# Encoder layer on one core: where a conditioning store is queued, the order of four prologue instructions, and the buffers of four rows at the end of the joint gate stage

## The chip, the core and the metric

The kernel runs on one NeuronCore of a Trainium2 chip. The core has TensorE (PE, matmuls; its weight loads are listed as PEld), VectorE (DVE), ScalarE (ACT), GpSimd (POOL) and SyncE (SP). SP issues most loads on a hardware queue (q1), POOL issues stores and some loads on a software queue (q0), ACT a few stores (q10). Three queues, sixteen DMA engines below them.

The metric is the device time of one execution in microseconds. A profiled execution adds a trace; its span is the time from its first to its last instruction.

## What is computed

One layer, width 1024, 1024 positions, everything float32 in and out:

```
mod = silu(c) @ w_ada + b_ada               # 6 columns of 1024: sh1 sc1 gt1 sh2 sc2 gt2
h   = rmsnorm(x, norm1_g) * (1 + sc1) + sh1
z   = h @ w_in                              # u v q k va gate_a gate_b
a   = gmlp(u, v) @ w_a;  b = window_attention(q, k, va) @ w_b
merged = sigmoid(gate_a) * a + sigmoid(gate_b) * b
x   = x + gt1 * (merged @ w_o)
h2  = rmsnorm(x, norm2_g) * (1 + sc2) + sh2
x   = x + gt2 * ((silu(h2 @ w_gate) * (h2 @ w_up)) @ w_out)
```

## The kernel before

**Numbers as pairs.** A float32 matrix product is made from pairs: a tile is cast to a rounded high part, and the low part is what the rounding left (`split`, `unit`). A product of two pairs is three matmuls: high by high, high by low, low by high. So each 128x1024 weight tile costs one cast on ACT (`wh<-raw`) and one subtraction on DVE (`wl<-raw,wh`) or POOL before PE can use it. The raw tile, the high part and the low part each have three buffers (tags `raw`, `wh`, `wl` of `wpool`).

**Who sets the order.** A planner turns the text into one instruction list for each engine. It lets an instruction run ahead of earlier text when its inputs and its buffer are there, unless the text pins it. `load` (line 137) issues a transfer from SP and pins it in SP's order. `store` (line 140) issues one from POOL and does not pin it; several loads go through `store` as well. Where `in_order[0]` is true, every DVE, ACT, POOL and PE instruction made through the wrappers stays in the order of the text. A tile that asks for a buffer of a tag waits until few enough earlier tiles of that tag are still in use.

**Prologue (lines 737 to 780, pinned).** The half of x that is worked on first comes in as eight 128x640 pieces (`xt`, `mid<-in_xT_dram`). ACT squares them, DVE sums the squares into `ss`, PE sums over partitions, ACT takes the square root (`root`, tile name `ms`), DVE takes its reciprocal (`rcol`), PE spreads it over partitions, and two ACT copies bring it to SBUF (`rb`, tile name `ss`). Meanwhile `silu_c` (the SiLU of c, repeated on all partitions) is there, and `ada_dot` (one 128x1024 DVE instruction) multiplies a 128x1024 row block of `w_ada` by it and sums: one column of `mod`. The blocks come in pairs of 1 MB (`ada_pair`), the scale's (SC1) in the first half and the shift's (SH1) in the second. `ada_end` is a one-column instruction that adds the bias.

**Projection loop (lines 795 to 854, pinned).** For each of eight k: scale `xt[k]` by the column of `mod` and by `rb` (DVE, 128x640), cast to a high part with the shift added (ACT), take the low part (DVE, `h<-mid,mod,h`), then the q and k/v matmuls of that k. Between them DVE makes the two dots of the next k, and in some steps the low part of a weight tile.

**Attention of the first half (lines 1052 to 1085).** Eight steps s, not pinned as a whole. In step 5 the text has the store of `silu_c` to `silu_d` in DRAM (512 KB, tile name `silu_d<-silu_c`), which the last stage of the kernel reads again.

**Joint gate stage (lines 1239 to 1327).** For each row block d = 2 to 7 the two sigmoid gates are computed with seven block products (`gate_step`, 12 matmuls each; after some of them `gate_evict` reads the sums) and `gating` writes two 128x512 results to DRAM, `md[0][d]` and `md[1][d]`. The two weight tiles of a d come in with `gate_load(d)` one d earlier and use two of the three `raw` buffers. During the stage `ada_half` streams further `w_ada` rows through the two buffers of the tag `hs`.

In its last row block, d = 7, the rows `md[0][0]` to `md[0][7]` are brought back as pairs for the output projection: `m_load` starts a load into an `hs` buffer through `store`, `m_split` casts and subtracts. Rows 0 and 1 are loaded first; each split of a row k in 0 to 3 starts the load of row k + 2; rows 6 and 7 need no load, since `gating` leaves them in SBUF. The splits of 0 to 3, 6 and the gating are pinned; those of 4, 5 and 7 are not. The first weight tile of the projection, `w_o[0]`, is asked for inside d = 7, and `w_o[1]` and on in the projection loop (lines 1345 on), where PE needs the rows 0 to 7 in order.

Of the kernel before, what the change touches and what calls it, by code (L numbers as in the profile page):

```python
# [8 lines left out]
F32 = mybir.dt.float32  # L9
# [7 lines left out]
P = 128  # L17
# [21 lines left out]
def kernel(  # L39
# [99 lines left out]
    def store(dst, src):  # L139
        nc.gpsimd.dma_start(dst, src)  # L140
# [66 lines left out]
    def ada_dot(r, col):  # L207
        V.scalar_tensor_tensor(
            out=r, in0=r, scalar=1.0, in1=silu_c, op0=ALU.mult, op1=ALU.mult,
            accum_out=acc_mod[:, col : col + 1],  # L210
        )

    def ada_end(col, gain=None):
        o = mod[:, col : col + 1]
        if gain is None:
            V.tensor_scalar(o, acc_mod[:, col : col + 1], bada[:, col : col + 1],
                            0.5 if GT1 <= col < SH2 else 1.0, op0=ALU.add, op1=ALU.mult)
        else:
            V.scalar_tensor_tensor(
                out=o, in0=acc_mod[:, col : col + 1], scalar=badap[:, col : col + 1],  # L220
                in1=gain, op0=ALU.add, op1=ALU.mult,
            )
# [509 lines left out]
    def half(hf):  # L732
# [4 lines left out]
        if hf == 0:  # L737
            in_order[0] = True
            xt = [midt(F32, 1) for _ in range(3)]
            xt = [xt[k // 3][:, 0, k % 3 * 640 : (k % 3 + 1) * 640] for k in range(KT)]  # L740
            hl4 = midt(F32R, 16)
            base_bias = bias_base()
            build_bias(*base_bias, range(7))
            A.activation(sm(QPK, "es"), ones[:, :QPK], AF.Silu)
            crow = load_cond()
            for k in range(KT):
                load(xt[k], xT[k * P : (k + 1) * P, :640])
            r = ada_pair(0)
            wq0, wk0 = raw_unit(w_q[0]), raw_unit(w_kv[0])
            cond = silu_rows(crow)  # L750
            ss = ss_tile()
            sqs = [midt(F32, 1)[:, 0, :] for _ in range(3)]
            for k in range(KT):
                sq = sqs[k // 3][:, k % 3 * 640 : (k % 3 + 1) * 640]
                A.activation(sq, xt[k], AF.Square)
                if k:
                    V.tensor_tensor(ss, prev if k == 1 else ss, sq, op=ALU.add)
                prev = sq
                if k == 1:
                    silu_cond(cond)  # L760
                    V.tensor_scalar(badap, bada, 1.0, None, op0=ALU.add)
                    build_bias(*base_bias, range(7, NH))
            total = at_bank()
            for i in range(NT + 1):
                T.matmul(total[:, i : i + 1], ss[:, i * P : (i + 1) * P], ones[:, 0:1], start=True,
                         stop=True)
            root = sm(5, "ms")
            A.activation(root, total[:, : NT + 1], AF.Sqrt, scale=1.0 / D, bias=epsc)
            ada_dot(r[:, 0, :], SC1)
            ada_end(SC1, g1c[:, 0:1])  # L770
            ada_dot(r[:, 1, :], SH1)
            V.reciprocal(rcol[0], root)
            wq = unit(None, V, wq0)
            wk = [wpool.tile([P, UNIT], F32R, tag=x, name=nm(x)) for x in ("wh", "wl")]
            A.copy(wk[0], wk0)
            r = ada_pair(1)
            ada_dot(r[:, 0, :], SC1 + 1)
            rb = ss_tile()
            A.copy(rb[:, :HALF], spread(rcol[0], NT))
            A.copy(rb[:, HALF:], spread(rcol[0][:, NT : NT + 1], 1))  # L780
            hH = [hid(), hid()]
            hL = [hid(), hid()]
        else:
            hH, hL = h_next
# [10 lines left out]
        for k in range(KT):  # L795
            if hf == 0:
                x = xt[k]
                h4 = hl4[:, k, :]
                sh = mod[:, SH1 + k : SH1 + k + 1]
                if 0 < k < KT - 1:  # L800
                    r = ada_pair(k + 1)
                V.scalar_tensor_tensor(out=x, in0=x, scalar=mod[:, SC1 + k : SC1 + k + 1], in1=rb,
                                       op0=ALU.mult, op1=ALU.mult)
                ada_end(SH1 + k)
                A.activation(hH[k // 4][:, k % 4, :], x[:, :HALF], AF.Identity, bias=sh)
                if k == 0:
                    V.tensor_tensor(wk[1], wk0, wk[0].bitcast(F32), op=ALU.subtract)
                A.activation(h4, x[:, HALF:], AF.Identity, bias=sh)
                A.activation(x[:, HALF:], x[:, HALF:], AF.Identity, bias=sh)
                G.tensor_tensor(hl4[:, KT + k, :], x[:, HALF:], h4.bitcast(F32), op=ALU.subtract)  # L810
                if 0 < k < KT - 1:
                    ada_dot(r[:, 0, :], SC1 + k + 1)
                V.scalar_tensor_tensor(out=hL[k // 4][:, k % 4, :], in0=x[:, :HALF], scalar=sh,
                                       in1=hH[k // 4][:, k % 4, :].bitcast(F32),
                                       op0=ALU.add, op1=ALU.subtract)
                if k < KT - 1:
                    ada_end(SC1 + k + 1, g1c[:, k + 1 : k + 2])
                    ada_dot(r[:, 1, :], SH1 + k + 1)
                store(x0d[k], x[:, :HALF])
                if k == 7:  # L820
                    for i in range(2):
                        x_square(i)
            else:
                if k == 0:
                    wq, wk = early.pop(0), early.pop(0)
            if k == 4:
                wk = unit(None, V, wk_raw)
            if k % 2 == 1 and k < KT - 1:
                wq_next = unit(w_q[(k + 1) // 2], V)
            if k == 3:  # L830
                wk_raw = raw_unit(w_kv[1])
            sts = [(hH[k // 4][:, k % 4, t * P : (t + 1) * P], hL[k // 4][:, k % 4, t * P : (t + 1) * P])
                   for t in range(NT)]
            ksts = sts + [(hl4[:, k, :], hl4[:, KT + k, :])] if hf == 0 else sts[1:]
            oq, ok = (k % 2) * 512, (k % 4) * 256
            q_parts = [(qps[t], sts[t], wq, oq, 512, True, True) for t in range(NT)]
            k_parts = [(kps[t], ksts[t], wk, ok, 256, hf == 1 or t == 4, hf == 1 or t % 2 or t == 4)
                   for t in range(nkv)]

            for group in ((q_parts, k_parts) if k == 4 else (q_parts + k_parts,)):  # L840
                for e in range(2):
                    for ps, st, w, o, n, first, last in group:
                        if e == 0:
                            T.matmul(ps, st[0], w[0][:, o : o + n], start=k == 0 and first, stop=False)
                            T.matmul(ps, st[0], w[1][:, o : o + n], start=False, stop=False)
                        else:
                            T.matmul(ps, st[1], w[0][:, o : o + n], start=False,
                                     stop=bool(k == KT - 1 and last))
            if hf == 1 and k in (2, 3):
                ada_half_load(("hs", "xs")[k % 2])  # L850
            elif hf == 1 and k > 3:
                ada_half(("hs", "xs")[k % 2] if k < 6 else None)
            if k % 2 == 1 and k < KT - 1:
                wq = wq_next
# [197 lines left out]
        for s in range(nw):  # L1052
# [8 lines left out]
            if hf == 0 and s == 7:  # L1061
                x_rstd()
            if hf == 0 and s == 5:
                store(silu_d, silu_c)
            normalise(sc[0], sc[2], den)
            if s == 0:
                end_unit()
# [172 lines left out]
    for d in range(2, KT):  # L1240
# [41 lines left out]
        if d > 2:  # L1282
            if last:
                m0.extend(m_tiles(midt))
                for k in range(2):
                    m_load(m0, 0, k)
                m_src[6] = tmp()
                gating(d - 1, None, m_src[6])
            else:
                gating(d - 1)  # L1290
# [5 lines left out]
        if not last:  # L1296
            gate_prep_a(d + 1)
        else:
            wo_next = unit(w_o[0], V)
            for k in (0, 1):  # L1300
                m_split(m0, k)
                m_load(m0, 0, k + 2)
        gate_step(d, 4)
        gate_evict(d, 4)
        if not last:
            gate_sums(d + 1)
            low_b, low_s = gate_prep_b(d + 1)
        else:
            m_split(m0, 6)
            for k in (2, 3):  # L1310
                m_split(m0, k)
                m_load(m0, 0, k + 2)
            m_src[7] = tmp()
            gating(d, 0, m_src[7])
        gate_step(d, 5)
# [666 lines left out]
```

## Time and profile before

| | |
|---|---|
| time, median of 3 runs | 1249.4 us (1247.3 to 1250.37) |
| the profiled execution | 1249.81 us |
| its span | 1248.0 us |
| granted TensorE clock | 1.000 |
| PE busy | 1219.6 us, 98% of the span |
| DVE busy | 915.1 us, 73% |
| ACT busy | 577.8 us, 46% |
| POOL busy | 184.0 us, 15% |
| DMA, mean over the span | 189 GB/s |

A row of the timeline is: start in us, duration in us, engine, line, operation, output and inputs by tile name, how many instructions are merged into the row, and in brackets the idle time before it and what ended that. Nearly all compute rows carry line 76, the wrapper that makes them, so they are told apart by tile names. A row of the waits is: who waited for whom, us in total, how many times, the longest. A row of the windows is: the stretch, its length, busy us (and instructions) of PE, PEld, DVE, ACT and POOL, the granted clock, the busy share of the DMA engines and the GB/s they moved.

### The profile page before, as it was taken

The numbers are of one execution on the slowest core, as the hardware profiler recorded it, in microseconds if no ns is written. First come the engines' busy times: TensorE is split into PE (matmuls) and PEld (weight loads), VectorE is DVE, ScalarE is ACT, GpSimd is POOL, SyncE is SP. The second block draws the span as 40 slices with busy tenths as digits, with TensorE's granted clock in tenths as the row PEclk, the third lists the DMA queues.
The fourth block names the chain that finished last, engine by engine and source line by source line (L and its number), as shares of the span: only waits on it lengthen the run. The fifth ranks groups of instructions, "written<-read, shape, count | busy, mean of one in ns | idle before, by whom it ended". The sixth has DMA issues, their size and how long they took to land.

```text
span 1248.0 us, 15657 instructions
## 1 busy us (share of the span) xinstructions
PE 1219.6 (98%) x5634; PEld 1008.8 (81%) x5634; DVE 915.1 (73%) x1548; ACT 577.8 (46%) x938; POOL 184.0 (15%) x234
## 2 busy tenths in 40 slices
PE   5999999999999999999999999999999999999998
PEld 3888888888887887788888887888888887888887
DVE  8997884487897798877797766765766666665746
ACT  5477864267876323434554333333333334433342
POOL 1223330023342010332100000010000000010001
PEclk9999999999999999999999999999999999999999
DMA  9721258431157466777503445455554459896642
GB/s 359 276 102 60 77 184 297 144 100 51 60 162 241 162 203 236 243 281 257 215 34 117 170 152 186 155 199 193 183 213 170 169 189 377 320 354 227 198 155 102
DMA packets 77664, 236.29 MB, mean 189 GB/s; under 512 B 9361, under 2 KB 9361, under 8 KB 71570
## 3 DMA queue, kind: packets, MB, share of 16 engines
q1 hardware_dynamic: 55298, 142.48, 32.9%
q0 software_dynamic: 18832, 86.52, 19.6%
q10 hardware_dynamic: 3456, 6.29, 1.3%
q8 instruction: 44, 0.72, 0.2%
q14 instruction: 34, 0.28, 0.1%
HBM read 177.58 MB, written 57.67 MB: 189 GB/s over the span
## 4 chain that ended last, share of the span: by engine, by line
PE 63%; DVE 12%; issue 11%; DMA 9%; ACT 3%; POOL 1%; SPq 0%; ACTq 0%; POOLq 0%; DVEq 0%
PE at L76 32%; PE mm L76 31%; DVE mid L76 3%; DVE wl L76 3%; ACT wh L76 2%; DMA wS<-wo 2%; DMA raw<-in_w_out_dram 1%; DMA raw<-in_w_ga_dram 1%; DMA wo<-in_w_out_dram 1%; DVE hs L76 1%; DMA mid<-in_w_ada_dram 1%; DVE t L76 1%; DVE ws L76 1%; DVE raw L76 1%; DVE xs L76 1%
## 5 line engine op out<-in xcount | busy, mean ns | idle before, releaser
L76 ACT CAST wh<-raw 128x1024 fp32r<-128x1024 f32 x155 | 162.4, 1051 | 146.5 <-PE mm L76 45.6
L76 DVE TENSOR_TENSOR wl<-raw,wh 128x1024 fp32r<-128x1024 f32 x141 | 171.9, 1221 | 71.1 <-ACT wh L76 68.4
L76 PE MATMUL mm<-mid,wh 128*128 128x512 f32 x696 | 215.7, 390 | 1.8 <-ACT mid L76 1.0
L76 PEld LDWEIGHTS mm<-mid,wh 128*128 128x128 f32 x696 | 130.3, 188 | 31.2 <-ACT mid L76 1.9
L76 PE MATMUL at<-j,wh 128*128 128x512 f32 x464 | 143.0, 389 | 0.0
L76 PE MATMUL mm<-mid,wl 128*128 128x512 f32 x348 | 135.4, 390 | 0.6 <-POOL wl L76 0.6
L76 PE MATMUL mm<-wh,h 128*128 128x512 f32 x384 | 128.8, 397 | 2.8 <-ACT h L76 2.7
L76 PEld LDWEIGHTS at<-j,wh 128*128 128x128 f32 x464 | 86.9, 188 | 18.5 <-ACT wh L76 0.4
L76 DVE TENSOR_TENSOR wl<-ws,wh 128x1024 fp32r<-128x1024 f32 (+1 forms) x55 | 62.0, 1127 | 43.9 <-ACT wh L76 43.9
L76 PE MATMUL at<-j,wl 128*128 128x512 f32 x232 | 90.4, 389 | 0.5 <-DVE wl L76 0.5
L76 PE MATMUL mm<-j,wh 128*128 128x512 f32 x288 | 89.0, 390 | 0.6 <-ACT wh L76 0.6
L76 PE MATMUL at<-h,wh 128*128 128x512 f32 x288 | 89.0, 390 | 0.0
L76 PEld LDWEIGHTS mm<-wh,h 128*128 128x128 f32 x384 | 71.2, 188 | 17.8 <-ACT h L76 4.1
L76 PE MATMUL mm<-h,wh 128*128 128x512 f32 x272 | 84.5, 392 | 0.0
L76 ACT CAST wh<-ws 128x1024 fp32r<-128x1024 f32 (+1 forms) x55 | 53.6, 974 | 59.3 <-DVE ws L76 43.5
L76 PEld LDWEIGHTS mm<-mid,wl 128*128 128x128 f32 x348 | 65.3, 188 | 14.4 <-POOL wl L76 1.0
L76 PE MATMUL mm<-wl,h 128*128 128x512 f32 x192 | 75.0, 391 | 0.0
L76 PEld LDWEIGHTS mm<-j,wh 128*128 128x128 f32 x288 | 53.8, 188 | 12.0 <-ACT wh L76 1.0
L76 PEld LDWEIGHTS at<-h,wh 128*128 128x128 f32 x288 | 53.8, 188 | 11.3 <-DVE mid L76 0.3
L76 PEld LDWEIGHTS mm<-h,wh 128*128 128x128 f32 x272 | 50.6, 188 | 10.3
L76 ACT ACTIVATE xs<-xs 128x512 f32<-128x512 f32 x21 | 13.3, 633 | 98.0 <-DVE xs L76 98.0
L76 DVE TENSOR_TENSOR ol<-raw,oh 128x1024 fp32r<-128x1024 f32 x30 | 36.5, 1223 | 27.8 <-ACT oh L76 27.3
(284 smaller groups left out, 2576.5 us busy)
## 6 DMA issues: line engine op xcount, KB each, us to landing
raw<-in_w_gate_dram SPq DMA_DIRECT2D x28, 512.0 KB, 5.1
tA<-hid POOLq DMA_DIRECT2D x11, 1024.0 KB, 4.9
tB<-hid POOLq DMA_DIRECT2D x11, 1024.0 KB, 5.0
wo<-in_w_out_dram POOLq DMA_DIRECT2D x22, 512.0 KB, 6.3
wS<-wo POOLq DMA_DIRECT2D x11, 1024.0 KB, 5.4
raw<-wS SPq DMA_DIRECT2D x44, 256.0 KB, 3.2
raw<-tB SPq DMA_DIRECT2D x44, 256.0 KB, 4.1
raw<-in_w_out_dram SPq DMA_DIRECT2D x33, 256.0 KB, 5.1
```

What stands on the lines that cost most here:

```text
L76: ins = f(*args, **kw)
```

## The change

Four edits in three places.

The store of `silu_c` in step 5 of the first attention half is made with `load` in place of `store`: it is issued by SP, pinned in SP's order, and no longer by POOL.

In the prologue, the reciprocal stands ahead of the dot of SH1 and no longer behind it. The dot of the second scale, SC1 + 1, leaves the place ahead of the copies into `rb`, and is made in step k = 0 of the loop, where the other steps have theirs, behind the first scaling.

In d = 7 of the joint stage, rows 2 to 5 are loaded at once behind rows 0 and 1, in pairs, into the two halves of two `raw` tiles of `wpool`. The loads that each split started are gone.

```diff
             ada_end(SC1, g1c[:, 0:1])
+            V.reciprocal(rcol[0], root)
             ada_dot(r[:, 1, :], SH1)
-            V.reciprocal(rcol[0], root)
             wq = unit(None, V, wq0)
...
             r = ada_pair(1)
-            ada_dot(r[:, 0, :], SC1 + 1)
             rb = ss_tile()
...
-                if 0 < k < KT - 1:
+                if k < KT - 1:
                     ada_dot(r[:, 0, :], SC1 + k + 1)
...
             if hf == 0 and s == 5:
-                store(silu_d, silu_c)
+                load(silu_d, silu_c)
...
                 for k in range(2):
                     m_load(m0, 0, k)
+                for k in (2, 4):
+                    r = wpool.tile([P, UNIT], F32, tag="raw", name=nm("raw"))
+                    for j in range(2):
+                        m_load(m0, 0, k + j, r[:, j * 512 : (j + 1) * 512])
                 m_src[6] = tmp()
...
             wo_next = unit(w_o[0], V)
             for k in (0, 1):
                 m_split(m0, k)
-                m_load(m0, 0, k + 2)
...
             m_split(m0, 6)
             for k in (2, 3):
                 m_split(m0, k)
-                m_load(m0, 0, k + 2)
             m_src[7] = tmp()
             gating(d, 0, m_src[7])
```

## The prediction

> **What bounds the kernel.** I read the page's shares first, then PE's waits over the whole span, then the timeline of the three places that the diff touches.
>
> ```profile
> PE 1219.6 (98%) x5634; PEld 1008.8 (81%) x5634; DVE 915.1 (73%) x1548; ACT 577.8 (46%) x938; POOL 184.0 (15%) x234
> ...
> PE at L76 <- DVE ss L76: 8.3, 1, 8.3
> PE at L76 <- DVE rcol L76: 2.3, 1, 2.3
> ```
>
> PE is busy for 1219.6 of 1248.0 us, so 28.4 us are all that a reordering can win. 12.4 us of it are three waits ahead of the first projection matmul (8.3 and 2.3 here, 1.8 at 24.03 below); most of the rest is some twenty short stalls. An edit counts only where PE stands still today, and behind each place PE is nearly gapless, so what it gains there is kept to the end.
>
> **The start.** The timeline of the prologue, all engines:
>
> ```profile
> 7.88 0.69 POOL L140 DMA_DIRECT2D silu_d<-silu_c  x1 [6.13 <-ACT silu_c L76]
> 9.68 4.54 DVE L76 TENSOR_TENSOR ss<-ss,mid 128x640 f32<-128x640 f32 x5 [0.63 <-ACT mid L76]
> 16.02 1.23 DVE L76 SCALAR_TENSOR_TENSOR mid<-mid,silu_c 128x1024 f32<-128x1024 f32 x1 [1.79 <-DMA mid<-in_w_ada_dram]
> 16.61 0.27 ACT L76 ACTIVATE ms<-at,epsc 128x5 f32<-128x5 f32 x1 [2.16 <-PE at L76]
> 17.42 1.22 DVE L76 SCALAR_TENSOR_TENSOR mid<-mid,silu_c 128x1024 f32<-128x1024 f32 x1
> 18.57 0.18 DVE L76 RECIPROCAL rcol<-ms 128x5 f32<-128x5 f32 x1
> 18.67 1.18 DVE L76 TENSOR_TENSOR wl<-raw,wh 128x1024 fp32r<-128x1024 f32 x1
> 18.90 2.48 PE L76 MATMUL at<-ident,rcol 128*128 128x128 f32 x10 [2.33 <-DVE rcol L76]
> 20.98 0.76 ACT L76 COPY ss<-at 128x512 f32<-128x512 f32 x2 [1.33 <-PE at L76]
> 21.06 1.22 DVE L76 SCALAR_TENSOR_TENSOR mid<-mid,silu_c 128x1024 f32<-128x1024 f32 x1 [1.21 <-DMA mid<-in_w_ada_dram]
> 22.21 0.88 DVE L76 SCALAR_TENSOR_TENSOR mid<-mid,mod,ss 128x640 f32<-128x640 f32 x1
> 24.03 0.50 PE L76 MATMUL mm<-wh,h 128*128 128x512 f32 x1 [1.80 <-ACT h L76]
> 26.41 0.87 DVE L76 SCALAR_TENSOR_TENSOR mid<-mid,mod,ss 128x640 f32<-128x640 f32 x1
> 33.57 0.50 PE L76 MATMUL mm<-wh,h 128*128 128x512 f32 x1 [0.19 <-ACT h L76]
> ```
>
> To see: DVE waits twice for `w_ada` (1.79 and 1.21 us); the square root is there at 16.88, yet its reciprocal starts at 18.57; the copies into `rb` end at 21.74, yet the scaling starts at 22.21, behind a dot whose data came at 21.06. And the store, written in attention, is issued at 7.88 already.
>
> ```profile
> 14.00:16.00 2.00, 1.72 (x8) 1.73 (x9) 0.22 (x1) 0.45 (x1) 0.00 (x0) 1.00 1.02 416
> 115.00:120.00 5.00, 5.00 (x30) 4.32 (x29) 4.17 (x14) 3.55 (x9) 1.34 (x2) 1.00 0.46 157
> silu_d<-silu_c POOLq DMA_DIRECT2D x1, 512.0 KB, 8.4
> 107.88 8.57 SPq L137 DMA_DIRECT2D hs<-in_xr_dram  x2
> 135.82 1.04 ACT L76 CAST wh<-raw 128x1024 fp32r<-128x1024 f32 x1
> ```
>
> The store leaves a stretch in which the DMA engines are full (share 1.02, 416 GB/s) and lands at 7.88 + 8.4 = 16.3 us. Its 0.52 MB at 416 GB/s are 1.26 us of all engines, nearly all moved before the first `w_ada` pair lands at 16.0. Without it I let that pair, and all loads behind it, land some 1.1 us sooner (ends: 0, and 1.26).
>
> First dot then: 16.02 - 1.1 = 14.9; with its closing column (17.42 - 16.02 = 1.40) DVE is free at 16.3. The root stays at 16.88: it hangs on the sums, which end at 9.68 + 4.54 = 14.22 and run back to back. So the reciprocal starts at about 16.95, 1.6 us sooner; spread and copies follow as they did (18.57 to 21.74 is 3.17 us): `rb` at 20.1. DVE meanwhile does the SH1 dot (1.15) and the low part (1.14), free at about 19.45, and idles 0.7 us where the removed dot stood. Then the scaling, and the dot behind it.
>
> From 21.06 to 26.41 no DVE row of the timeline has idle time; the same 5.35 us of work now start at 20.15. Gain 0.9 us. PE's first matmul comes 2.1 us sooner (22.21 + 1.82 = 24.03 becomes 20.15 + 1.82), but in the loop PE waits for ACT behind DVE (33.57, 0.19), so it keeps DVE's 0.9 only. Ends: if `rb` came no sooner, the scaling would start at 21.74 and DVE lose 0.7; if `rb` were there when DVE is free, 1.6 gained. If the store is not what delays the pair, the reciprocal is at 17.45, the scaling at 20.65, and 0.4 is gained. I take 0.9, since the full DMA share is measured.
>
> The 8.4 us to landing mean that the store moved at some 62 GB/s beside q1's loads. The Trainium skill, page "DMA: Bandwidth & Descriptors", section "Queues, rings and completion order", says that each DMA engine takes turns between the queues that have work, a packet at a time. By that the store would have had about half the engines and been through in some 3 us (an estimate); the trace does not bear that out. The sum by the rule would be 4.1 in place of 3.5, and it is the last rival's mechanism.
>
> Where the store goes: SP, in step 5, behind the second x load of the row 107.88, so near 116.5 us. It waits for nothing. SP spends one issue (some 0.4 us, as its neighbours) and the engines 1.26 us, at a share of 0.46. Queued behind it is a weight tile that ACT casts at 135.82. I cost the move at nothing; with that cover gone it would be 1.7 us. POOL loses one issue of 0.69, and has no other work there.
>
> **The joint stage's last row block.** PE first, then those it waits for:
>
> ```profile
> 512.67 0.39 PE L76 MATMUL mm<-mid,wl 128*128 128x512 f32 x1
> 513.65 0.50 PE L76 MATMUL mm<-mid,wh 128*128 128x512 f32 x1 [0.60 <-ACT mid L76]
> ...
> 514.72 0.40 PE L76 MATMUL mm<-mid,wl 128*128 128x512 f32 x1
> ...
> 517.46 0.73 PE L76 MATMUL at<-h,wh 128*128 128x512 f32 x2
> ...
> 520.95 0.50 PE L76 MATMUL mm<-mid,wh 128*128 128x512 f32 x1 [0.45 <-ACT mid L76]
> ...
> 522.01 0.40 PE L76 MATMUL mm<-mid,wl 128*128 128x512 f32 x1
> 512.99 1.24 ACT L76 CAST mid<-hs 128x512 fp32r<-128x512 f32 x2 [1.89 <-DMA hs<-md]
> 513.63 1.32 DVE L76 TENSOR_TENSOR mid<-hs,mid 128x512 fp32r<-128x512 f32 x2 [1.81 <-ACT mid L76]
> 516.73 0.68 DVE L76 TENSOR_TENSOR mid<-mid,at 128x512 f32<-128x512 f32 x1
> ```
>
> PE stands twice: for rows 2 and 3, and for rows 4 and 5. A matmul of this shape follows the one before by 0.23 us (below, 492.49 to 492.95 for two). From 512.67 to 514.72 three steps take 2.05 where 0.69 would do: 1.36 lost. At the second place 0.45 idle, and 520.95 to 522.01 takes 1.06 for two steps in place of 0.46: 1.05 lost, and the restart of 517.46 and of 520.95 some 0.1 each (0.50 for a first matmul, 0.39 for a next one). Together 2.6.
>
> When do the rows come now? That hangs on the three `raw` buffers:
>
> ```profile
> 489.25 1.05 ACT L76 CAST wh<-raw 128x1024 fp32r<-128x1024 f32 x1 [5.40 <-DMA raw<-in_w_ga_dram]
> 489.71 6.60 SPq L137 DMA_DIRECT2D raw<-in_w_o_dram  x2
> 499.08 1.22 DVE L76 TENSOR_TENSOR wl<-raw,wh 128x1024 fp32r<-128x1024 f32 x1 [0.26 <-ACT wh L76]
> 500.33 0.33 SPq L137 DMA_DIRECT2D raw<-in_w_o_dram  x1
> 504.07 1.04 ACT L76 CAST wh<-raw 128x1024 fp32r<-128x1024 f32 x1
> raw<-in_w_o_dram SPq DMA_DIRECT2D x4, 512.0 KB, 4.1
> 492.49 0.62 PE L76 MATMUL mm<-mid,wh 128*128 128x512 f32 x2
> 492.95 0.39 PE L76 MATMUL mm<-mid,wl 128*128 128x512 f32 x1
> ```
>
> Buffers go in the order of the text, each when one comes free: today `w_o[0]` takes the third at 489.71, `w_o[1]` the next at about 496, `w_o[2]` the last one of d = 7 at 500.33, right behind the low part of 499.08. Two tiles of rows now stand ahead. Rows 2 and 3 take the third buffer, free by 489.71 at the latest (near 482, I think, when d = 6 is through with it); rows 4 and 5 the one of 496; `w_o[0]` that of 500.33, 10.6 us later than today. The four `w_o` loads here land after 4.1 us (median): 504.4, 0.3 behind the cast of 504.07, and PE wants it at 511.5 only. `w_o[1]` takes the buffer of `w_o[0]` near 508.1 and lands by 513; PE wants it behind the last gate product.
>
> So all four rows are in SBUF at about 501. Their casts need no wait: rows 4 and 5, unpinned, fit ACT's and DVE's gaps near 507 and 510; 2 and 3 follow row 6 on ACT, low parts by 513.1, as PE reaches them. DVE loses its 1.81 us, the gating behind it moves up, and with it the eviction of 516.73 that frees the last gate product (517.46). PE then has `w_o[0]` with rows 0 to 7, the gate product, and `w_o[1]`, in a row. I take the whole 2.6. Ends: -1.4 (third rival), and 2.6; no more, since no other PE wait here depends on these rows. POOL issues the same four loads of 256 KB, queued ahead of x's rows and rows 0 and 1, with nothing urgent behind. If the stall goes, next late is `w_o[1]`.
>
> The trade: rows 2 and 3 (0.52 MB) may share the engines with `w_ga` of d = 7, which ACT awaits at 489.25. PE needs its low part, ready near 491.5, at 492.95: 1.4 us of room. At 416 GB/s the two rows are 1.26 us, inside it, so nothing; at the 157 GB/s of the thin stretch above it would be 3.3, and cost 1.9.
>
> **Sum.** 0.9 + 2.6 = 3.5 us off the profiled execution's 1249.81 (span 1248.0 and 1.81 around it): 1246.3. That execution lies 0.4 above the median: 1245.9.
>
> **Rivals.**
> *Rows come early, but PE stands for something else.* The eviction or `w_o[1]` comes after PE has done rows 0 to 6, and 2 of the 2.6 us return: 1247.9. For it: `w_o[1]` starts 12 us later than today. Against: it is needed only after eight rows and a gate product.
> *The start gives nothing back.* `rb` stays where it was, DVE idles for it, 0.7 lost in place of 0.9 gained: 1247.5. Against: the square root waits 1.7 us for its reciprocal.
> *Slower: `w_o[0]` is late.* ACT and DVE run in written order here, so a late cast of `w_o[0]` pushes everything behind it:
>
> ```profile
> DMA to landing us min/median/max: 3.6/7.9/8.6
> ```
>
> At the slowest landing of a `w_o` load, 8.6, it is there at 508.9, 4.8 behind today's cast. Row 2's low part slides from 512.4 to 517.2 while PE has used rows 0 and 1 by 513.2: a stall of 4.0 against 2.6 now. Minus the start's 0.9, 0.5 slower: 1249.9. It decides from a landing of 8.1 us on.
> *The store's move does nothing* (0.4 at the start): 1246.4, inside my range.
> *The store holds up x's pieces, not `w_ada`.* Then, without it, DVE's 0.63 of idle ahead of 9.68 goes too, sums and root come that much sooner, and the reciprocal, which hangs on the root, with them: 4.1 us, 1245.3. Against: the store is issued at 7.88 only, and lands behind all of x.
>
> **Chances.** Forecast 0.57 (alone 1244.6 to 1247.2; the store's 0.4 case is in it), PE stands elsewhere 0.12, nothing at the start 0.07, slower 0.14, x's pieces 0.10. 0.3% is 3.7 us, about what a measurement of this kernel can tell from no change: faster is below 1245.65, slower above 1253.1. Given how single runs spread (1247.3 to 1250.37 before), faster gets half of the forecast (0.285), most of the x's-pieces case (0.09), and 0.055 from the other cases' lower ends: 0.43; slower by that much needs the late `w_o[0]` and 3 us more, as from a `w_ga` that is late as well: 0.10. Within: 0.47. Range 1243.6 (the last rival and 1.7 of spread) to 1249.4 (short of the slower rival).
>
> **What would show it.** The store from SP near 116 us; first DVE dot near 14.9, reciprocal near 17.0, scaling near 20.2, PE at 22.0; the scaling of k = 1 near 25.5. Four `md` loads into `raw` before 497, `w_o[0]` issued near 500; no PE wait on `mid` between 505 and 515. Wrong if PE waits there for `wh` or `wl` of `w_o`, if `w_ga` of d = 7 lands after 490.6, or if k = 1's scaling is not before 26.

## The result, and the profile after

The changed kernel takes 1244.96 us (median of 11 runs, 1242.88 to 1247.07), the kernel before on the same chip 1248.63 us (11 runs): ratio 0.997, 95% interval 0.9959 to 0.998. That is 3.7 us less; the forecast was 3.5 us less, 1245.9. The profiled execution took 1245.15 us, with a span of 1243.3, 4.7 below the one of before. Single executions spread by some 2 us either way, and so do single traces, so what follows leans on what repeats over several of them.

The page, and then the longest waits of PE over the whole span:

```profile
PE 1220.3 (98%) x5634; PEld 1010.6 (81%) x5634; DVE 914.7 (74%) x1548; ACT 577.3 (46%) x938; POOL 183.6 (15%) x233
```

```profile
PE at L76 <- DVE ss L76: 7.5, 1, 7.5
...
PE at L76 <- DVE rcol L76: 0.7, 1, 0.7
```

PE is as busy as before; its wait for the square sums is 0.8 us shorter and that for the reciprocal 1.6. The start of the changed kernel, DVE's timeline:

```profile
8.12 5.47 DVE L76 TENSOR_TENSOR ss<-ss,mid 128x640 f32<-128x640 f32 x6 [0.21 <-ACT mid L76]
13.81 1.23 DVE L76 SCALAR_TENSOR_TENSOR mid<-mid,silu_c 128x1024 f32<-128x1024 f32 x1 [0.21 <-DMA mid<-in_w_ada_dram]
...
16.28 0.19 DVE L76 RECIPROCAL rcol<-ms 128x5 f32<-128x5 f32 x1 [0.98 <-ACT ms L76]
16.38 1.19 DVE L76 SCALAR_TENSOR_TENSOR mid<-mid,silu_c 128x1024 f32<-128x1024 f32 x1
...
19.49 0.89 DVE L76 SCALAR_TENSOR_TENSOR mid<-mid,mod,ss 128x640 f32<-128x640 f32 x1 [0.77 <-ACT ss L76]
...
21.55 1.22 DVE L76 SCALAR_TENSOR_TENSOR mid<-mid,silu_c 128x1024 f32<-128x1024 f32 x1
...
24.83 0.87 DVE L76 SCALAR_TENSOR_TENSOR mid<-mid,mod,ss 128x640 f32<-128x640 f32 x1
```

The first dot comes at 13.81 us (before 16.02) and no longer waits 1.79 us for its data. The new idle time is the thing to see: 0.98 us ahead of the reciprocal, for the root, and 0.77 ahead of the scaling, for `rb`. The scaling of k = 1 is at 24.83 (before 26.41).

The joint stage of the changed kernel, POOL and SP first, then ACT, DVE and PE:

```profile
480.37 0.54 POOL L140 DMA_DIRECT2D raw<-md  x1 [13.51 <-DVE wl L76]
...
486.71 0.54 POOL L140 DMA_DIRECT2D raw<-md  x1
494.21 1.07 POOL L140 DMA_DIRECT2D raw<-md  x2 [6.96 <-DVE wl L76]
498.85 57.91 SPq L137 DMA_DIRECT2D raw<-in_w_o_dram  x12
486.68 1.05 ACT L76 CAST wh<-raw 128x1024 fp32r<-128x1024 f32 x1 [3.78 <-DMA raw<-in_w_ga_dram]
505.45 1.14 ACT L76 CAST mid<-raw 128x512 fp32r<-128x512 f32 x2
509.57 1.14 ACT L76 CAST mid<-raw 128x512 fp32r<-128x512 f32 x2
510.61 1.04 ACT L76 CAST wh<-raw 128x1024 fp32r<-128x1024 f32 x1
510.30 1.29 DVE L76 TENSOR_TENSOR mid<-raw,mid 128x512 fp32r<-128x512 f32 x2
514.38 0.68 DVE L76 TENSOR_TENSOR mid<-mid,at 128x512 f32<-128x512 f32 x1
515.53 0.39 PE L76 MATMUL mm<-mid,wh 128*128 128x512 f32 x1
515.76 0.61 PE L76 MATMUL at<-h,wh 128*128 128x512 f32 x2
```

The four rows go out before 496 us, `w_o[0]` at 498.85, and the casts of rows 2 to 5 (`mid<-raw`) have no idle time in front of them. `w_ga` of d = 7 is cast at 486.68, sooner than before. PE has no wait between 500 and 530 us; the gate product starts at 515.76, 0.23 us behind the matmul ahead of it.

One wait is new:

```profile
214.46 0.86 SPq L137 DMA_DIRECT2D xs<-in_w_ada_dram  x2
220.23 0.69 DVE L76 SCALAR_TENSOR_TENSOR xs<-xs,silu_c 128x512 f32<-128x512 f32 x1 [6.22 <-DMA xs<-in_w_ada_dram]
220.85 1.22 DVE L76 TENSOR_TENSOR wl<-raw,wh 128x1024 fp32r<-128x1024 f32 x1
222.12 0.50 PE L76 MATMUL mm<-wl,h 128*128 128x512 f32 x1 [0.72 <-DVE wl L76]
```

In the projection loop of the second half, DVE stands 6.22 us for a `w_ada` transfer, and behind it in DVE's list is the low part of `w_q[1]`, which PE wants. Before, PE came 1.5 us later, and just too late to notice.

To follow the gain along the span I compare the start of the same matmul (both traces have 5634) with the kernel before. Negative is ahead of before, in us; the time at the head is that of the matmul in the kernel before. The lower rows are the experiments.

| kernel | 62.8 | 217.2 | 239.2 | 393 | 493 | 523 | 1231 |
|---|---|---|---|---|---|---|---|
| changed | -1.61 | -1.51 | -0.47 | -0.51 | -1.44 | -4.26 | -4.62 |
| changed_again | -0.57 | -0.58 | +0.03 | +0.04 | +0.02 | -2.79 | -2.74 |
| only_store | -1.98 | -1.87 | -0.57 | -0.48 | -0.42 | -1.48 | -2.93 |
| only_order | +0.32 | +0.42 | +1.47 | +1.54 | +1.21 | +0.97 | +0.11 |
| only_rows | -0.61 | -0.55 | -0.15 | -0.07 | -0.71 | -3.53 | -4.16 |
| one_tile | +0.44 | +0.38 | +0.80 | +0.84 | -0.46 | -3.18 | -0.72 |
| low_first | -1.59 | -1.52 | -1.53 | -1.52 | -3.69 | -6.51 | -6.37 |
| low_first_2 | -1.33 | -1.29 | -1.30 | -1.25 | -3.27 | -6.09 | -6.13 |
| recip_back | -1.56 | -1.49 | -1.50 | -1.47 | -2.71 | -5.52 | -5.16 |
| no_reorder | -2.38 | -2.41 | -2.43 | -2.38 | -2.73 | -5.54 | -6.32 |
| no_reorder_2 | -1.76 | -1.69 | -1.70 | -1.67 | -2.00 | -4.82 | -5.19 |
| dot_back | -1.59 | -1.51 | -1.51 | -1.51 | -2.18 | -5.00 | -5.81 |
| dot_back_2 | -2.48 | -2.43 | -2.44 | -2.42 | -1.78 | -4.60 | -3.95 |

The first row is the result in short: 1.6 us at the start, of which 1.0 is given back at 222 us; 2.8 us between 493 and 523, kept; the rest is smaller and differs from trace to trace. One stretch is not explained: between 239 and 493 us, most of it behind 393, the traces gain up to 2.2 us (low_first) and lose up to 0.7 (dot_back_2) against the one trace of before. No edit was aimed at that stretch, and what comes and goes there is as large as several of the effects below.

### The profile page after: what moved, and what is told of

Its sections match the earlier page's. It is cut to its first block, busy times and chain, and to the rows that moved or that the text cites. A ratio compares the mean times of both kernels' runs of the same rounds, so it can differ in the third digit from the quotient of the medians.

```text
span 1243.3 us, 15662 instructions
## 1 busy us (share of the span) xinstructions
PE 1220.3 (98%) x5634; PEld 1010.6 (81%) x5634; DVE 914.7 (74%) x1548; ACT 577.3 (46%) x938; POOL 183.6 (15%) x233
## 4 chain that ended last, share of the span: by engine, by line
PE 71%; DVE 11%; issue 9%; DMA 4%; ACT 3%; POOL 0%; SPq 0%; ACTq 0%; DVEq 0%; POOLq 0%
PE mm L76 36%; PE at L76 35%; DVE mid L76 3%; DVE wl L76 2%; ACT wh L76 2%; DMA wo<-in_w_out_dram 1%; DMA wS<-wo 1%; DVE hs L76 1%; DMA raw<-in_w_ga_dram 1%; DMA xs<-x1sd 1%; DVE t L76 1%; DVE ws L76 1%; DVE xs L76 1%; DVE raw L76 1%; ACT lb L76 1%
## 5 line engine op out<-in xcount | busy, mean ns | idle before, releaser
L76 PEld LDWEIGHTS at<-j,wh 128*128 128x128 f32 x464 | 86.9, 188 | 18.6 <-ACT wh L76 0.4
L76 PEld LDWEIGHTS mm<-mid,wl 128*128 128x128 f32 x348 | 65.3, 188 | 14.6 <-POOL wl L76 1.0
L76 PEld LDWEIGHTS at<-h,wh 128*128 128x128 f32 x288 | 53.9, 188 | 11.1
L76 ACT ACTIVATE xs<-xs 128x512 f32<-128x512 f32 x21 | 13.3, 632 | 96.8 <-DVE xs L76 96.8
L76 PE MATMUL mm<-j,wl 128*128 128x512 f32 x144 | 56.2, 390 | 0.5 <-DVE wl L76 0.5
```

The lines of the kernel that those rows point to most:

```text
L76: ins = f(*args, **kw)
```

## The experiments

Theory A: the store's place delayed the first loads, and with it gone the rest of the prologue hangs on the square sums; of the lead that this gives, the place at 222 us lets about 0.5 us through; the rows at once take away both stalls of the joint stage. The rival held in the prediction: store and reordering give about half of the start's gain each, and all of it is kept.

### Each part alone

**The store alone.**

```diff
             if hf == 0 and s == 5:
-                store(silu_d, silu_c)
+                load(silu_d, silu_c)
```

> The kernel before with the store edit alone. Theory A (the store holds up x's pieces and the first w_ada pair, and in the changed kernel this alone brought the start forward): DVE's idle ahead of the square sums is gone, the sums end near 13.6 us, the first dot is near 13.8, the reciprocal, though still behind the SH1 dot, near 16.4, the scaling of k = 1 at 24.8 to 25.2 (before 26.41), and PE stands 1.2 to 1.6 us ahead at 62 us. Of this about 1.0 is given back at 222 us, as in the changed kernel, where a low part waits behind a dot for a w_ada transfer that does not come sooner; the time ends 0.4 to 0.7 below the kernel before. Rival B (the prediction's split: the store gives the pair 1.1, the order the rest): first dot near 14.9, reciprocal 17.45, scaling of k = 1 near 25.9, PE 0.5 ahead at 62 us, all of it kept: 0.5 below. The end times do not tell them apart, the starts do. Rival C: the sooner x pieces in the changed kernel were chance of that run; then the sums end at 14.2 here.

Measured: ratio 0.9987 (0.9978 to 0.9996), 1.6 us less, more than the 0.4 to 0.7 expected; the interval reaches down to 0.5. DVE's timeline at the start:

```profile
14.15 1.22 DVE L76 SCALAR_TENSOR_TENSOR mid<-mid,silu_c 128x1024 f32<-128x1024 f32 x1 [0.30 <-DMA mid<-in_w_ada_dram]
15.56 1.22 DVE L76 SCALAR_TENSOR_TENSOR mid<-mid,silu_c 128x1024 f32<-128x1024 f32 x1
16.70 0.18 DVE L76 RECIPROCAL rcol<-ms 128x5 f32<-128x5 f32 x1
...
19.11 1.22 DVE L76 SCALAR_TENSOR_TENSOR mid<-mid,silu_c 128x1024 f32<-128x1024 f32 x1 [0.41 <-DMA mid<-in_w_ada_dram]
20.26 0.88 DVE L76 SCALAR_TENSOR_TENSOR mid<-mid,mod,ss 128x640 f32<-128x640 f32 x1
...
24.46 0.88 DVE L76 SCALAR_TENSOR_TENSOR mid<-mid,mod,ss 128x640 f32<-128x640 f32 x1
```

The store's move alone brings PE 1.98 us forward at 62.8 us: more than all three edits of the start together in the changed kernel. B falls: the reordering is not what made the gain possible. The SH1 dot now fits into the wait for the root, and the dot of SC1 + 1 has its data at 19.1 and fits into the wait for `rb`. At 222 us 1.3 of the 1.9 us are given back, more than expected.

Why the store's removal is worth more than its bytes shows in the windows view of 10 to 14 us, here of the kernel before and then of only_store (the last columns are the share and the rate of the DMA engines):

```profile
10.00:14.00 4.00, 0.00 (x0) 0.00 (x0) 3.58 (x5) 3.48 (x5) 0.00 (x0) 1.00 1.03 375
```

```profile
10.00:14.00 4.00, 0.09 (x1) 0.09 (x1) 3.44 (x5) 3.49 (x4) 0.00 (x0) 1.00 1.02 425
```

The engines are full in both, but they move 375 GB/s with the early store and 425 without. Over all traces: 363 to 391 in the four kernels with the early store, 423 to 428 in the ten traces without. The DMA view tells when the loads lose. Its rows are queue, packets, MB and share of the engines, q1 for the loads and q0 for the store: the kernel before from 10 to 12 us, the same from 12 to 16, and only_store from 10 to 12:

```profile
q1 hardware_dynamic: 168, 0.70, 108.8%
```

```profile
q1 hardware_dynamic: 227, 1.11, 67.2%
q0 software_dynamic: 144, 0.52, 32.0%
```

```profile
q1 hardware_dynamic: 175, 0.89, 106.5%
```

The store is issued at 7.88 us, yet no packet of it is on record ahead of 12.26; its last one starts at 15.6. So the loads lose twice. From 10 to 12 us, ahead of the store's first packet, the full engines move 0.19 MB less than in only_store. From 12 to 16 us they move nearly as much as without the store (409 and 423 GB/s), but 0.52 MB of it is the store's. Together that is 0.7 MB, or 1.7 us at 416 GB/s (an estimate from these rows), and the first dot moved by 1.87, from 16.02 to 14.15. That the lower rate ahead of the store's packets comes from the store is shown: only_store differs from the kernel before in nothing else, and no trace overlaps (327 to 384 GB/s from 10 to 12 us in the four with the early store, 438 to 450 in the ten without). How the store does it without a packet is not shown.

The first dot starts at 16.02, 16.80, 14.77 and 16.57 us with the early store (mean 16.0), and at 13.5 to 14.8 in the ten without (mean 14.0).

C is not settled. The square sums end at 14.15 to 15.45 us with the early store (mean 14.7) and at 13.4 to 14.6 without it (mean 13.8). The means point to x's pieces being held up too, by some 0.8 us, but single traces overlap. The packet records say the same: the last packet of x ends at 11.1 to 13.3 us with the early store (mean 12.3) and at 10.6 to 12.0 without (mean 11.2). That is the stretch of the lower rate, and in two of the four traces it is over before the store's first packet.

**The reordering alone.**

```diff
+            V.reciprocal(rcol[0], root)
             ada_dot(r[:, 1, :], SH1)
-            V.reciprocal(rcol[0], root)
...
             r = ada_pair(1)
-            ada_dot(r[:, 0, :], SC1 + 1)
...
-                if 0 < k < KT - 1:
+                if k < KT - 1:
```

> The kernel before with the two prologue reorderings alone, the store left where it was. Both theories: the first dot stays at 16.0 us, the reciprocal comes at 17.45, the copies into rb end at 20.65, the scaling starts there and no longer at 22.21, and DVE keeps 0.4 us at 62 us; the time is 0.4 below. If the second w_ada pair (landing 21.06) then delays the moved dot, the gain is smaller, 0.1 to 0.3. Theory A adds: 0.4 fits under the 0.5 us that the place at 222 us lets through, so it is kept to the end. If the reordering were the source of the 1.6 us seen in the changed kernel, PE would stand more than 1 us ahead at 62 us.

Measured: ratio 0.9997 (0.9987 to 1.0007): no difference. In its trace the first pair happened to land late, at 16.80; counted from the first dot, the scaling of k = 1 comes 9.94 us later, against 10.39 in the kernel before. That agrees with the 0.4 us, but it does not show in the time, and the trace loses 1.05 us at 222.

**The rows alone.**

```diff
                 for k in range(2):
                     m_load(m0, 0, k)
+                for k in (2, 4):
+                    r = wpool.tile([P, UNIT], F32, tag="raw", name=nm("raw"))
+                    for j in range(2):
+                        m_load(m0, 0, k + j, r[:, j * 512 : (j + 1) * 512])
```

with the loads behind each split gone.

> The kernel before with the joint stage's edit alone. Theory A: PE loses the two stalls on rows 2, 3 and 4, 5 and gains 2.6 to 2.9 us between 500 and 525 us, keeps them, and with the 0.35 us that vanished near 765 us if that belongs to this edit, the time is 2.6 to 3.2 below the kernel before (0.9974 to 0.9979). The w_ga tile of d = 7 lands no later than in the kernel before (cast at 489.25). Rival: part of the changed kernel's gain between 400 and 520 us came from the start's lead; then this kernel gains under 2 us. Rival from the prediction: w_o[0] or w_ga late: a stall on wh or wl between 485 and 525.

Measured: ratio 0.9982 (0.9974 to 0.9991), 2.2 us less, where 2.6 to 3.2 were expected. PE gains 2.82 us from 493 to 523 us, as in the changed kernel, and keeps it; it has no wait between 500 and 530 us. Neither rival holds. Every trace with this edit gains 2.81 or 2.82 in that stretch: PE is gapless there. The kernel before varies: only_store and only_order, which have the old rows, gain 1.06 and 0.24 against the trace of before in the same stretch. Against the mean of the three traces with the old rows the edit is worth 2.4 us.

**One raw tile in place of two.**

```diff
+                r = wpool.tile([P, UNIT], F32, tag="raw", name=nm("raw"))
+                for j in range(2):
+                    m_load(m0, 0, 2 + j, r[:, j * 512 : (j + 1) * 512])
...
             for k in (0, 1):
                 m_split(m0, k)
-                m_load(m0, 0, k + 2)
+                m_load(m0, 0, k + 4)
```

> The kernel before with only rows 2 and 3 loaded at once into a raw tile; rows 4 and 5 are loaded into the buffers that rows 0 and 1 leave, where rows 2 and 3 were loaded before. By the prediction's terms the stall on rows 2 and 3 (1.4 us) goes, and rows 4 and 5, which then land where 2 and 3 landed (512.9 us) and are needed only behind the gate product, no longer stop PE either: 2.4 to 2.9 us gained between 500 and 536 us. Rival: rows 4 and 5 need a buffer ahead as well; then 1.2 to 1.6 us are gained, and a wait of PE on mid stays near 518 us.

Measured: 2.72 us gained from 493 to 523, so in this trace one tile is enough for both stalls. The time does not confirm that the gain is kept: ratio 0.9988 (0.9975 to 1.0001). In this trace 3.2 us are lost again behind the stage, on a weight tile of the next output projection:

```profile
558.58 0.73 PE L76 MATMUL mm<-j,wh 128*128 128x512 f32 x2 [0.68 <-ACT wh L76]
560.98 0.50 PE L76 MATMUL mm<-j,wl 128*128 128x512 f32 x1 [1.67 <-DVE wl L76]
```

Whether that belongs to this order of the buffers or to the one execution, one trace can't tell. recip_back and dot_back_2 lose 1.3 and 0.9 us between 523 and 564 as well, with two tiles; the other traces with two tiles lose nothing. It stays open.

### The place at 222 us

The changed kernel, with a dependence of issue order that puts the low parts of `w_q[1]` and `w_q[2]` ahead of the dots that wait for `w_ada`. No other engine's list changes.

```diff
     def unit(src, eng=None, raw=None):
...
-        (eng or V).tensor_tensor(l, r, h.bitcast(F32), op=ALU.subtract)
+        low_of[0] = (eng or V).tensor_tensor(l, r, h.bitcast(F32), op=ALU.subtract)
...
     def ada_half(more=None):
...
-            V.scalar_tensor_tensor(out=t[i], in0=t[i], scalar=1.0,
+            ins = V.scalar_tensor_tensor(out=t[i], in0=t[i], scalar=1.0,
...
+            after(ins, hold[0])
+        hold[0] = None
...
                 wq_next = unit(w_q[(k + 1) // 2], V)
+                low_q[k] = low_of[0]
...
             elif hf == 1 and k > 3:
+                hold[0] = low_q.get(k - 4) if k % 2 else None
                 ada_half(("hs", "xs")[k % 2] if k < 6 else None)
```

> The changed kernel, with the low parts of the two weight tiles w_q[1] and w_q[2] of the second projection loop put ahead of the dots that wait for w_ada (DVE runs its list in order). Theory A (the start's lead of 1.6 us is cut to 0.5 at 222 us by this order alone): the wait of 0.72 us of PE on wl at 222.12 is gone, PE keeps 1.5 us at 250 us, and the time is 0.7 to 1.1 below the changed kernel, near 1244.0 (ratio to the kernel before 0.996). Rival: the lead runs into the next thing that does not move with it (a transfer or a buffer at 300 to 480 us), PE's lead at the end of the joint stage is no larger than in the changed kernel, and the time is the same, 1245.

Measured: 1244.48 us, ratio 0.9968 (0.9956 to 0.998). DVE's timeline (its instructions carry line 77 here):

```profile
214.22 1.23 DVE L77 TENSOR_TENSOR wl<-raw,wh 128x1024 fp32r<-128x1024 f32 x1 [0.24 <-ACT wh L77]
219.74 0.69 DVE L77 SCALAR_TENSOR_TENSOR xs<-xs,silu_c 128x512 f32<-128x512 f32 x1 [4.29 <-DMA xs<-in_w_ada_dram]
```

The low part is made at 214.22, in the time in which DVE stood idle, and PE waits for nothing between 200 and 240 us. Theory A holds in the traces: from 217 to 239 us the seven traces with this edit keep their lead to 0.02 us. The six traces without it, other than that of the kernel before, lose 0.40 to 1.30 there, only_order too, although its PE comes later than in the kernel before: the landing of the transfer varies, and the kernel before was profiled in an execution in which it was just in time. In the time, the edit's gain is within what can be told: the 14 runs of this kernel stand 0.4 below the 17 of the changed kernel, give or take 1.0.

The changed kernel once more, beside the next experiments:

> The changed kernel once more, beside the others on one chip. Its time is 0.3 to 0.5% below the kernel before, as it was; PE about 1.6 us ahead at 62 us and about 0.5 us ahead at 250 us, with a wait of about 0.7 us on wl near 222 us. If that wait is chance, it is not there in this run, and the lead stays at 1.6 us.

Measured: 1244.96 us, ratio 0.9969 (0.9956 to 0.9981). Its lead at 62.8 us is 0.57 only, since the square sums ended at 14.61 in this execution and not at 13.59. The wait at 222 us is there (0.28 us, 0.6 given back). The 1.61 of the first trace was thus in good part a draw.

### Which reordering costs

only_store was ahead of the changed kernel at the start, so the reordering looked like a loss once the store is gone. Four corners, all with the store moved, the rows at once and the low parts first. **no_reorder** has neither reordering, **dot_back** only the reciprocal's, **recip_back** only the dot's, low_first both.

```diff
-            V.reciprocal(rcol[0], root)
             ada_dot(r[:, 1, :], SH1)
+            V.reciprocal(rcol[0], root)
...
             r = ada_pair(1)
+            ada_dot(r[:, 0, :], SC1 + 1)
...
-                if k < KT - 1:
+                if 0 < k < KT - 1:
```

That is no_reorder against low_first; recip_back has the first two lines of it, dot_back the rest.

> The kernel low_first without the two prologue reorderings: the store's move, the rows at once, and the low parts first. Theory A (with the store out of the way the root is what the prologue waits for, and the reordering makes DVE stand 0.98 us for the root and 0.77 us for rb where the old order had the two dots to do): the start is that of only_store, scaling of k = 1 near 24.4 us, PE 1.9 to 2.0 us ahead at 62 us against 1.6 in low_first, kept to the end; the time is 0.3 to 0.4 below low_first, near 1244.1. Rival: the 0.4 us between only_store and the changed kernel was chance of one run (the landing of the second w_ada pair); then PE stands 1.4 to 1.7 us ahead at 62 us.

> The kernel low_first with the dot of SC1 + 1 back ahead of the copies into rb, the reciprocal still ahead of the SH1 dot. Theory A (the dot's move is what costs, since its data is there by 19.1 us and DVE stands idle for rb until 19.5; the reciprocal's place then decides nothing, because the scaling waits for that dot): scaling of k = 0 at 20.2 us, of k = 1 near 24.4, PE 1.9 to 2.0 us ahead at 62 us. Rival (the reciprocal ahead of the dot costs, by its 0.98 us of standing): as in low_first, 1.6 us ahead.

> The kernel low_first with the reciprocal back behind the SH1 dot, the dot of SC1 + 1 still in the loop. Theory A (the dot's move costs 0.6 us, the reciprocal's place next to nothing): the scaling of k = 1 stands 11.1 to 11.6 us behind the end of the square sums, as in the changed kernel (11.24), against 10.5 to 10.7 where the dot is back; the time is that of low_first within 0.4%, 0.3 to 0.8 us above no_reorder. Rival (the reciprocal's place costs, the dot's move does not): 10.5 to 10.7 us, and the time of no_reorder.

> The kernel no_reorder once more, beside the other three corners. Theory A: scaling of k = 1 at 10.5 to 10.7 us behind the end of the sums; time 1243.3 to 1244.3, the lowest of the four together with dot_back. If 1243.4 was a low draw, it comes out near 1244.5.

> The kernel dot_back once more. Theory A: 10.6 to 10.7 us behind the end of the sums, and, since nothing else differs, the time of no_reorder within 0.5 us: the 1.9 us between the two in the run before were the landing of x's pieces and other draws. Rival: the reciprocal's place costs 1 to 2 us by a way that the first 62 us do not show; then the time is 1245 again.

> The kernel low_first once more. Theory A: 11.2 to 11.3 us behind the end of the sums; PE keeps its start lead past 222 us; time 0.5 to 0.7 above no_reorder, near 1244.4. Rival: no difference from no_reorder in time, the lead of the start being lost later on.

DVE at the start in no_reorder, then dot_back_2, then recip_back:

```profile
16.27 0.19 DVE L77 RECIPROCAL rcol<-ms 128x5 f32<-128x5 f32 x1
...
18.71 1.23 DVE L77 SCALAR_TENSOR_TENSOR mid<-mid,silu_c 128x1024 f32<-128x1024 f32 x1 [0.31 <-DMA mid<-in_w_ada_dram]
19.86 0.88 DVE L77 SCALAR_TENSOR_TENSOR mid<-mid,mod,ss 128x640 f32<-128x640 f32 x1
...
24.06 0.87 DVE L77 SCALAR_TENSOR_TENSOR mid<-mid,mod,ss 128x640 f32<-128x640 f32 x1
```

```profile
16.12 0.19 DVE L77 RECIPROCAL rcol<-ms 128x5 f32<-128x5 f32 x1 [1.01 <-ACT ms L77]
...
18.59 1.23 DVE L77 SCALAR_TENSOR_TENSOR mid<-mid,silu_c 128x1024 f32<-128x1024 f32 x1
19.74 0.88 DVE L77 SCALAR_TENSOR_TENSOR mid<-mid,mod,ss 128x640 f32<-128x640 f32 x1
...
23.94 0.88 DVE L77 SCALAR_TENSOR_TENSOR mid<-mid,mod,ss 128x640 f32<-128x640 f32 x1
```

```profile
16.33 0.19 DVE L77 RECIPROCAL rcol<-ms 128x5 f32<-128x5 f32 x1
...
19.54 0.88 DVE L77 SCALAR_TENSOR_TENSOR mid<-mid,mod,ss 128x640 f32<-128x640 f32 x1 [1.05 <-ACT ss L77]
...
24.88 0.88 DVE L77 SCALAR_TENSOR_TENSOR mid<-mid,mod,ss 128x640 f32<-128x640 f32 x1
```

The end of the square sums varies by chance; the distance from there to the scaling of k = 1 hardly does (us, one value for each trace; only_store and the changed kernel have the same start as no_reorder and low_first):

| | dot of SC1 + 1 ahead of the copies | in the loop |
|---|---|---|
| reciprocal behind the SH1 dot | 10.61, 10.51, 10.53 | 11.24 |
| reciprocal ahead of it | 10.67, 10.50 | 11.24, 11.23, 11.24, 11.24 |

So the dot's move costs 0.7 us and the reciprocal's place nothing: the rival on the reciprocal falls. By its lead alone (1.59 at 62.8 us) the first trace of dot_back reads like that rival; its sums ended late, at 14.16, and from there it has 10.67. With the dot moved, DVE idles 0.77 or 1.05 us for `rb`; with the dot in its old place that time is filled, and the scaling stands only some 0.4 us behind `rb`. PE takes over what DVE has: its lead at 62.8 us is 26.41 less the start of the scaling of k = 1, to 0.04 us, in all ten traces without the early store.

The times: no_reorder 1243.42 and 1243.68 us (ratios 0.9957, 0.9944 to 0.997, and 0.9959, 0.9945 to 0.9973), dot_back 1245.31 and 1244.27, low_first 1244.48 and 1244.37, recip_back 1245.35. All runs with the dot ahead stand 0.7 us below those with the dot in the loop (25 runs each, give or take 0.7), which is the trace's number. But the times alone would not carry it. no_reorder and dot_back, which have the same start, differ by 1.2 us (13 and 12 runs, give or take 0.8), though under 0.5 was expected; with the dot in the loop the difference between the same two places of the reciprocal has the other sign (0.8 us by the means); and recip_back stands 1.7 us above no_reorder_2, where 0.3 to 0.8 was expected. Where these differences come from is not shown. That the dot's move costs rests on the traces.

no_reorder has the lowest time of all: 1.3 us below the changed kernel (13 and 17 runs, give or take 0.9), and 5.5 and 4.9 below the kernel before.

## Why the prediction was right, and where not

The larger term, the joint stage, is right in its mechanism. The smaller one, the start, is not: the store gave more than forecast, the reordering took some of it back, and of what was left (1.61 and 0.57 us in the two traces of the changed kernel) 1.0 and 0.6 were lost at 222 us, a place the prediction did not look at. That the sum comes within 0.2 us of the measured difference is in part luck.

- **The joint stage, 2.6: right in mechanism, size 2.4 to 2.8.** All four rows went out where the buffers were expected, `w_o[0]` left at 498.85 (forecast 500.33), `w_o[1]` was cast at 510.61, and PE has no wait. The trade with `w_ga` cost nothing. The slower rival (`w_o[0]` late) and the one with PE standing elsewhere did not come. What the prediction did not consider: by the trace of one_tile one of the two tiles takes away both stalls.
- **The first pair, 1.1 us sooner, ends 0 and 1.26: too small.** It came 2.0 us sooner on average. The store's own bytes, 1.26 us, moved ahead of the pair as assumed. The term left out is the stretch before them: the prediction read the full share in the windows from 14 us on and did not look at the rate from 10 to 12, where the kernel before moves 348 GB/s and the changed one 450, at a share of 1.09 and 1.08.
- **"the store moved at some 62 GB/s": a wrong reading, on which the sum does not hang.** The 8.4 us from issue to landing hold 4.4 us without a packet. The 0.52 MB then moved in 3.3 us, some 157 GB/s, so the estimate of some 3 us was right for the moving, and the trace does bear out the turns between the queues (last section).
- **The root stays at 16.88: not so.** It hangs on the sums as said, but these move from execution to execution by a microsecond, and come sooner on average without the store. The last rival (x's pieces) is borne out in its direction, with 0.8 us between the means, and not settled.
- **From the sums on: right.** The forecast put the scaling of k = 1 at 25.5 with sums ending at 14.22, 11.28 us apart; the two traces of the changed kernel have 11.24 and 11.23.
- **What the reordering is worth: wrong.** The prediction gave it 0.4 of the 0.9 (its case in which the store delays nothing). The step that failed is that the old order was never carried through with the store gone, and that "and idles 0.7 us where the removed dot stood" was written down and not priced as a place in which the dot could stand. By its own numbers the second pair lands at 20.0, the dot in its old place ends at 21.1, and the scaling of k = 1 follows 4.20 us behind that (22.21 to 26.41 before), at 25.3; with the reordering it forecast 25.5. In the runs the pair lands by 18.6 to 19.5, and with the old order and the store gone the start gains 0.7 more.
- **"what it gains there is kept to the end": wrong for the start.** PE is gapless behind it because the kernel before was just in time at 222 us in its trace. There a transfer's landing, not PE, sets when a low part is made, so the lead is cut to what that leaves: 0.5 in the changed kernel's trace, and nothing in its second.
- **The store on SP at no cost: right.** It was issued at 114.92 us for 0.43 us, and no lead changes by more than 0.03 us between 108 and 131 us in any trace that has it.

By what the traces show for its two terms the sum would have been 0 to 0.5 and 2.4 to 2.8 us, 2.4 to 3.3; the time says 3.7, with an interval of 2.5 to 5.1. So the forecast of 3.5 stands nearer to the time than its terms account for, and the rest is not assigned.

## What to carry to other kernels

Before moving an instruction out of an idle engine's way, ask what the engine will do instead: an instruction whose data is there costs nothing ahead of a wait, and its full length behind it. A lead won early can end at the next place where an engine's list has an instruction that waits for a transfer in front of one that the bound engine needs; look through the timeline for such places, also where they cost nothing today. And judge a transfer among full DMA engines by the rate that they reach and by when its packets move: the time from issue to landing can hold a long stretch in which it moves nothing.

## What the runs showed of the hardware

**A store on the software queue moves nothing for over 4 us, and then takes turns with the loads.** In the four traces with the early store its first packet is on record 4.2 to 4.4 us behind the issue and its last starts 3.0 to 3.8 us later; the 8.0 to 8.9 us from issue to landing are therefore no measure of its rate. From 10 to 12 us, ahead of its first packet, the full engines moved 327 to 384 GB/s in these traces and 438 to 450 in the ten others. The Trainium skill, page "DMA: Bandwidth & Descriptors", section "Queues, rings and completion order", has each engine take turns between its queues, a packet at a time. The trace of the kernel before agrees: from 12.5 to 13.5 us it has 36 packets of the store and 35 of the loads (0.15 and 0.29 MB), from 14 to 15 us 50 and 53 (0.20 MB each).

**PE at half its rate at a granted clock of 1.00.** The first projection matmuls of the changed kernel, and then of its second trace:

```profile
21.31 0.79 PE L76 MATMUL mm<-wh,h 128*128 128x512 f32 x1 [1.36 <-ACT h L76]
21.90 0.63 PE L76 MATMUL mm<-wl,h 128*128 128x512 f32 x1
22.32 0.63 PE L76 MATMUL mm<-wh,h 128*128 128x512 f32 x1
```

```profile
22.32 0.50 PE L76 MATMUL mm<-wh,h 128*128 128x512 f32 x1 [1.47 <-ACT h L76]
22.66 0.40 PE L76 MATMUL mm<-wl,h 128*128 128x512 f32 x1
22.89 0.39 PE L76 MATMUL mm<-wh,h 128*128 128x512 f32 x1
```

In the first the matmuls of 512 columns follow each other by 0.42 to 0.43 us, and those of 256 columns behind them by 0.21, until 26.1; in the second it is 0.23 and 0.12 from the start, though the kernel is the same. Of the 14 traces six run at full rate from the first of these matmuls on, and eight are slow for some 3 to 5 us, two of them (only_store, only_rows) after a few matmuls at full rate. The windows view gives a granted clock of 1.00 for all of it. The Trainium skill, page "TensorE: Matmul & The Clock Gate", section "What's actually happening", explains such a thing by a gate that looks at PE's activity in windows of 3.4 us which run freely, so that it depends on the phase; its spacing for a cold array at 512 columns, 426.7 ns (section "Wait — 56ns, not 53.3ns?"), agrees with the 0.43 here. No run here shows the gate itself. The slow stretch costs nothing in this kernel, since PE is ahead of DVE in these microseconds: the leads at 62.8 us follow DVE's scaling whether PE began slow or not.
